# A hybrid trunk in split fp32 on one core: PSUM tiles and weights of the last plain down block, and the buffers of three norms

## The chip, the core and the metric

The kernel runs on one core of one Trainium2 chip. The metric is the device time of one execution in microseconds (us), the median of several runs. The engines are named as in the profile: PE (TensorE), PEld (PE's weight loads), DVE (VectorE), ACT (ScalarE), POOL (GpSimd) and SP (SyncE, which here issues the DMAs). A difference of 0.3% (7.3 us) is about the least that a measurement of this kernel tells from no change.

## The reference

Two layers over 1024 tokens and 16 learned meta tokens, with a model width of 1024: a token mixer (differential attention in layer 0, a gated short convolution in layer 1), then an MLP with a squared ReLU. An RMS norm stands before and after each of them.

```python
def _rmsnorm(x, g):
    y = x * lax.rsqrt(jnp.mean(x * x, axis=-1, keepdims=True) + RMS_EPS)
    return y * g

def _short_conv(h, w_in, conv_w, w_out):
    b_gate, c_gate, u = jnp.split(jnp.einsum('bld,de->ble', h, w_in), 3, axis=-1)
    u = c_gate * u
    y = lax.conv_general_dilated(u, conv_w[:, None, :], window_strides=(1,), padding=[(CONV_WIDTH - 1, 0)], ...)
    return jnp.einsum('bld,de->ble', b_gate * y, w_out)

def _sqrelu_mlp(h, w_up, w_down):
    a = jax.nn.relu(jnp.einsum('bld,df->blf', h, w_up))
    return jnp.einsum('blf,fd->bld', a * a, w_down)

    for i in range(DEPTH):
        h = _rmsnorm(hres, norm_g[i, 0])
        m = _diff_attention(...) if i % N_MIXERS == 0 else _short_conv(...)
        hres = hres + _rmsnorm(m, norm_g[i, 1])
        h = _rmsnorm(hres, norm_g[i, 2])
        hres = hres + _rmsnorm(_sqrelu_mlp(h, w_up[i], w_down[i]), norm_g[i, 3])
    return hres[:, N_META:]
```

The inner width of the MLP is 4096.

## The kernel before

**Products.** Everything lies with the features on the 128 partitions and the tokens along the free axis, so a row (`row(m, c, s)`) is one of 8 blocks of 128 features. Each fp32 operand is split in two fp32r parts, `hi` (a rounded copy) and `lo` (the rest), and a product of 128x128 weights is three matmuls: hi·hi, hi·lo, lo·hi (`product`, L180). `up` products run over 8 blocks of features (24 matmuls), `dn` products over 4 (12 matmuls). Weights are read in tiles of 128x1024 (`w_raw`, one buffer in each pool), cast to `w_hi` by ACT (L149), and `w_lo` is subtracted by DVE (L150). Tokens are worked on in three chunks, in layer 0 of 344, 344 and 340 columns (`cut0`), called chunk 0, 1 and 2 here.

**Stages.** Attention of layer 0, `project_out` (L399, products `mo`), a norm, MLP 0, a norm, the convolution's three input projections (`conv_in`, products `cg`, `ug`, `bg`), `project_out` again, a norm, MLP 1, the last norm. An MLP (`mlp`, L613 on) runs one block of four `up` tiles (`up_plain`) and writes it to DRAM, 12 pairs of `up` tiles (`up_pair`), and another plain block, whose down products open `acc`. Then `Sevens.run` makes the 6 large down blocks as seven block products each (`pa`, `pb`, `pc`) in 24 steps `q`, in each of which DVE adds seven results to `acc` (L588). A weight tile of a step is loaded two steps ahead (`fetch`), into the raw buffer of the pool `wp` for an even `q` and of `wd` for an odd one. Last comes `down_plain` for the block written to DRAM (`done0` and `done1` add its products to `acc` and sum the squares for the norm that follows).

**PSUM.** `psum_stage` sets which tiles rotate. In `psp1`, of layer 0's block products and of the last down block after them, tiles are 1024 wide, two banks each: two of `a`, one each of `b` and `c`. `down_plain` takes them in the order a, b, a, c, and the sums over partitions (`total`, a matmul with a matrix of −1) use tag `c` too. `psp2`, from `conv_in` on, has eight tiles of one bank: `mm` 2, `s` 3, `t` 2 for products and `o` for sums.

**Norms.** `norm_step` (L372) is called once per chunk when the last row of a mixer or MLP is there. PE sums the squares over partitions (`mss` or `ass`), ACT and DVE make the root's inverse (`rsqrt_mean`, L190), then for each of 8 rows: DVE scales it (L389), DVE adds the residual (L390, from tiles `st` loaded by SP, two rows each), ACT makes the `hi` part `HH` for the next product (L391), DVE the `lo` part `HL` (L392), ACT a square `sq` (L211), which POOL adds to `ssn` or `rs` for the next norm (L212). The squares for `mss` or `ass` are made the same way after each `mo` or last `dn` product. Both kinds take their `sq` from one ring of two buffers. `add` is due at once and its second sum (`close`) 15 us later on a clock that counts matmuls.

**What sets the order.** Within `Sevens.run` PE's order is that of the code. Elsewhere a scheduler places each engine's instructions by a simulated timeline and the availability of buffers, so pools and rings shift instructions against each other. After that, each engine runs its list in order, and waits where an operand is missing. 

The closing lines of a down block in layer 0 are these:

```python
    def done0(mi, cols, am, ps):
        nc.vector.tensor_add(am, am, ps)
        add_square(mp, ass[:, cols[0] : cols[0] + cols[1]], am, mi == 0, cols[1])
        if mi == KC - 1:
            norm_step(mp, 0, 3, acc, ass, cols, ...)

    down_plain(acc, *last, list(range(FB)), cut0, done0)
    psum_stage("psp2", BANKS, 512, ROUND, "o")
```

## Time and profile before

| | us |
|---|---|
| median of 3 runs | 2448.94 (2444.61 to 2450.77) |
| the profiled execution | 2453.48 |
| its span | 2451.7 |
| PE busy in it | 2358.9 |
| DVE, ACT, POOL busy | 1483.7, 996.2, 433.1 |
| mean granted clock of PE | 0.983 |

A row of the timeline reads: start, duration, engine, line, operation, out<-in by the program's names (without the numbers of buffers), shapes, how many alike follow each other, and in brackets the idle time of the engine before it and who ended it. A row of the windows reads: the stretch, its length, the busy time of PE, PEld, DVE, ACT and POOL with the number of instructions, PE's granted clock, the DMA engines' busy share and GB/s. A row of groups has a count, the busy time and mean ns of one, and the idle time before. PE runs in order, so an idle time in its rows is one in which its next instruction waited; a matmul's duration overlaps the next one's, so the pace is read from starts.

### The profile page before, as it was taken

The page shows a single profiled execution, that of the slowest core. Times are in us where ns is not written, and L with a number is a line of the kernel's source. Part 1 is how long each engine was busy: PE and PEld are TensorE (multiplying, and loading weights), DVE is VectorE, ACT ScalarE, POOL GpSimd, SP SyncE. Part 2 cuts the span into 40 slices and gives each one's busy share as a digit, 9 for nine tenths or more (in the row PEclk, how much of TensorE's full clock was granted, in tenths as well). Part 3 has the DMA queues.
Part 4 walks back from the last instruction along what each step waited for, and adds up shares of the span by engine and source line. Part 5 has one row for each costly group of instructions (what it writes and reads, how often), then busy time and mean ns, then how long its engine had stood idle before and what let it go on. Part 6 is the DMA issues. An engine that isn't in the chain of part 4 may idle for free.

```text
span 2451.7 us, 36477 instructions
## 1 busy us (share of the span) xinstructions
PE 2358.9 (96%) x14330; PEld 2215.5 (90%) x14330; DVE 1483.7 (61%) x2655; ACT 996.2 (41%) x1893; POOL 433.1 (18%) x438
## 2 busy tenths in 40 slices
PE   8999999999899999999997799999899999999997
PEld 7899999999799999999996799999788888888887
DVE  7887777764855455366666644332755555367766
ACT  7776677764533333312214422223533333222215
POOL 3211111103300000133314300002400000132316
PEclk9999999999999999999998899999999999999999
DMA  4212222333365564577542311111456555476652
GB/s 133 66 53 61 62 61 61 101 112 115 101 231 187 220 226 170 194 265 271 202 147 92 98 44 52 44 65 42 125 192 229 203 194 223 172 292 238 225 197 70
DMA packets 110108, 357.67 MB, mean 146 GB/s; under 512 B 11120, under 2 KB 55536, under 8 KB 102768
## 3 DMA queue, kind: packets, MB, share of 16 engines
q1 hardware_dynamic: 109936, 355.33, 40.9%
q8 instruction: 113, 1.85, 0.3%
q14 instruction: 59, 0.48, 0.1%
HBM read 225.94 MB, written 120.84 MB: 141 GB/s over the span
## 4 chain that ended last, share of the span: by engine, by line
PE 81%; DVE 10%; ACT 4%; issue 2%; DMA 2%; POOL 1%; SPq 0%; DVEq 0%; POOLq 0%; ACTq 0%
PE up L187 27%; PE pa L565 11%; PE pb L565 6%; PE dn L187 5%; PE mo L187 4%; PE cg L187 4%; PE ug L187 4%; PE bg L187 4%; PE pc L565 3%; PE po L1272 2%; DVE HL L392 1%; PE tr L1233 1%; PE s L1186 1%; DMA w_raw<-in_wall 1%; PE s L1187 1%
## 5 line engine op out<-in xcount | busy, mean ns | idle before, releaser
L187 PE MATMUL up<-HL,w_hi 128*128 128x344 f32 (+3 forms) x1312 | 455.9, 348 | 6.4 <-DVE HL L392 6.2
L187 PEld LDWEIGHTS up<-HL,w_hi 128*128 128x128 f32 x1312 | 248.5, 189 | 30.1 <-DVE HL L392 9.4
L150 DVE TENSOR_TENSOR w_lo<-w_raw,w_hi 128x1024 fp32r<-128x1024 f32 (+1 forms) x119 | 147.8, 1243 | 209.8 <-ACT w_hi L149 209.6
L149 ACT CAST w_hi<-w_raw 128x1024 fp32r<-128x1024 f32 (+2 forms) x143 | 148.4, 1040 | 297.4 <-PE up L187 146.8
L187 PE MATMUL up<-HH,w_hi 128*128 128x344 f32 (+1 forms) x768 | 246.7, 323 | 7.1 <-ACT HH L391 4.7
L456 DVE SCALAR_TENSOR_TENSOR r<-up,ssn 128x344 f32<-128x344 f32 (+3 forms) x164 | 92.9, 571 | 254.9 <-PE up L187 254.7
L187 PE MATMUL up<-HH,w_lo 128*128 128x344 f32 (+1 forms) x768 | 245.7, 321 | 0.0
L543 POOL TENSOR_TENSOR s_tmp<-w_raw 128x256 f32<-128x256 f32 x48 | 35.8, 747 | 1016.7 <-DMA w_raw<-in_wall 769.5
L187 PEld LDWEIGHTS up<-HH,w_hi 128*128 128x128 f32 x768 | 145.2, 189 | 8.1 <-ACT HH L391 5.3
L187 PEld LDWEIGHTS up<-HH,w_lo 128*128 128x128 f32 x768 | 145.1, 189 | 0.4 <-DVE w_lo L150 0.2
L535 ACT CAST s_hi<-s_tmp 128x1024 fp32r<-128x1024 f32 x48 | 50.4, 1049 | 162.3 <-PE pb L565 147.2
L1196 ACT ACTIVATE E<-E,mn 16x16 f32<-16x16 f32 (+5 forms) x144 | 105.3, 732 | 24.4 <-DVE mn L1191 23.7
L187 PE MATMUL up<-YHa,w_hi 128*128 128x512 f32 (+2 forms) x272 | 104.6, 386 | 4.4 <-ACT YHa L391 4.4
L212 POOL TENSOR_TENSOR mss<-mss,sq 128x344 f32<-128x344 f32 (+2 forms) x42 | 41.8, 1001 | 372.0 <-ACT sq L211 371.4
L187 PE MATMUL up<-YHa,w_lo 128*128 128x512 f32 (+2 forms) x272 | 104.7, 385 | 0.0
L187 PE MATMUL up<-YHb,w_lo 128*128 128x512 f32 (+2 forms) x272 | 103.8, 382 | 0.0
L187 PE MATMUL up<-YHb,w_hi 128*128 128x512 f32 (+2 forms) x272 | 103.4, 380 | 0.0
L187 PE MATMUL mo<-HL,w_hi 128*128 128x342 f32 (+2 forms) x312 | 99.6, 319 | 0.0
L150 POOL TENSOR_TENSOR w_lo<-w_raw,w_hi 128x1024 fp32r<-128x1024 f32 (+1 forms) x24 | 57.5, 2397 | 201.7 <-ACT w_hi L149 179.1
L1191 DVE CUSTOM_DVE_ANT_0 E<-s,G 16x16 f32<-16x16 f32 (+5 forms) x144 | 64.5, 455 | 42.9 <-PE s L1187 40.9
L588 DVE TENSOR_TENSOR acc<-acc,pa 128x512 f32<-128x512 f32 x96 | 65.9, 686 | 32.8 <-PE pa L565 31.2
L535 ACT CAST a_hi<-w_raw 128x512 fp32r<-128x512 f32 x48 | 29.7, 620 | 136.2 <-DMA w_raw<-in_wall 127.3
(498 smaller groups left out, 7292.5 us busy)
## 6 DMA issues: line engine op xcount, KB each, us to landing
w_raw<-in_wall SPq DMA_DIRECT2D x189, 512.0 KB, 3.7
seven_dram<-stage SPq DMA_DIRECT2D x12, 2056.0 KB, 6.4
seven_dram<-stage SPq DMA_DIRECT2D x12, 2048.0 KB, 6.3
fx<-seven_dram SPq DMA_DIRECT2D x42, 514.0 KB, 6.9
fx<-seven_dram SPq DMA_DIRECT2D x42, 512.0 KB, 7.0
seven_dram<-stage SPq DMA_DIRECT2D x12, 1542.0 KB, 9.3
seven_dram<-stage SPq DMA_DIRECT2D x12, 1536.0 KB, 8.7
HL<-seven_dram SPq DMA_DIRECT2D x21, 514.0 KB, 7.9
```

Of the source, the lines that this page charges most:

```text
L149: nc.scalar.copy(hi_part, raw[:, cols])
L150: (eng or nc.vector).tensor_sub(lo_part, raw[:, cols], hi_part.bitcast(F32))
L187: nc.tensor.matmul(ps, lhs[:, a:b], rhs(k, cols), start=n == 0, stop=n == last)
L212: (eng or nc.gpsimd).tensor_add(ss, ss, sq)
L456: nc.vector.scalar_tensor_tensor(r, ps, 0.0, rs[:, c0 : c0 + n], ALU.max, ALU.mult)
L535: nc.scalar.copy(hl[0], src)
L543: nc.gpsimd.tensor_add(s1, a21, a22)
L565: nc.tensor.matmul(ps[:, off : off + n], lhs[:, a : a + P], F[j][slot][:, t, c : c + n], start=first and k == 0, stop=k == 5, skip_group_c ...
L588: nc.vector.tensor_add(am, am, got)
L1191: nc.vector.tensor_tensor_reduce(out=e[:rows, p0 : p0 + n], in0=ps[:rows], in1=self.G[:rows, off : off + n], scale=-(2.0 ** -(h + 1)), sca ...
L1196: nc.scalar.activation(e[:rows, :ext], e[:rows, :ext], AF.Exp, scale=-1.0, bias=mn, accum_out=H["sums"][:rows, c : c + 1])
L1272: nc.tensor.matmul(po[:, a0:ncols], v[:, j], a[:, j, a0:ncols], start=j == 0 and z == 0, stop=j == nch - 1 and z == 2)
```

## The change

Four things, in both layers where both have them:

1. `psp2` opens before layer 0's last down block and not after it. Its `dn` products rotate over seven single banks, and the sums have the eighth.
2. The four weight tiles of the last down block are loaded and split by `take_last` in the last two steps of `Sevens.run` (two in each), in halves of 128x512, into buffers that are free by then (`a_hi`/`a_lo`, `s_tmp`, `w_hi`/`w_lo` of `wp`). The pool `wd` stays open for it until `down_plain` is through. So `wx` opens later, and `shift` sets which of the two pools the first conv weights come from. In layer 1 this is all that changes at the down block.
3. The squares made within `norm_step` have a ring of their own (tag `sqn`), apart from those of the products before. The two norms after the mixers load the residual four rows at a time (`wide` 4, two buffers), the norm after layer 0's MLP two rows at a time as before.
4. `rsq` of the convolution uses the tile `ass`, `mlp0b` lies on the right side, and closes after the convolution.

```diff
     def load_weights(eng=None, raw=None, spare=None, early=None):
-        src = wpools[max(i - 3 * HEADS - EARLY + 1, 0) // 2 % len(wpools)]
+        src = wpools[(max(i - 3 * HEADS - EARLY + 1, 0) // 2 + shift[0]) % len(wpools)]
...
     def norm_step(..., wait, wide):
-                for c2 in (c4, c4 + 2):
-                    st = tp.tile([P, 2, n], F32, tag="st", name=f"st_{count[0]}_{c2}", bufs=3)
-                    nc.sync.dma_start(st, res_in(slice(c2, c2 + 2), s))
-                    for c in (c2, c2 + 1):
+                for c2 in range(c4, c4 + 4, wide):
+                    st = tp.tile([P, wide, n], F32, tag="st", name=f"st_{count[0]}_{c2}", bufs=2 if wide == 4 else 3)
+                    nc.sync.dma_start(st, res_in(slice(c2, c2 + wide), s))
+                    for c in range(c2, c2 + wide):
...
-                        add_square(tp, ssn[:, s], mc, c == 0, n)
+                        add_square(tp, ssn[:, s], mc, c == 0, n, tag="sqn")
...
-    def down_plain(acc, fh, fl, group, chunks, done):
-        ws = [weights() for _ in group]
+    def down_plain(acc, fh, fl, group, chunks, done, ws=None):
+        ws = ws or [[(w, 0), (w, FB * P)] for w in [weights() for _ in group]]
...
+        def take_last(self, i):
+            _, raw = self.take(4 * NW + i)
+            halves = [slice(0, 4 * P), slice(4 * P, 8 * P)]
+            def half(t):
+                return self.wd.tile([P, 4 * P], F32R, tag=f"a_{t}", name=f"last_{t}{i}_{count[0]}", bufs=3)
+            if i == 1:
+                ws = [[half("hi"), half("lo")] for _ in halves]
+            elif i == 3:
+                hi = self.wd.tile([P, 1024], F32R, tag="s_tmp", name=f"last_hi{count[0]}", bufs=1)
+                ws = [[hi[:, s], half(t)] for s, t in zip(halves, ("hi", "lo"))]
+            else:
+                w = [wp.tile([P, 1024], F32R, tag=f"w_{t}", name=f"last_{t}{i}_{count[0]}") for t in ("hi", "lo")]
+                ws = [[t[:, s] for t in w] for s in halves]
+            for w, s in zip(ws, halves):
+                self.split(w, raw[:, s])
+            self.last.append([(w, 0) for w in ws])
...
                 for q in range(n + 1):
                     if q + 2 < n:
                         self.fetch(q + 2)
+                    elif q == n - 1:
+                        self.take_last(0)
+                        self.take_last(1)
+                    elif q == n:
+                        self.take_last(2)
+                        self.take_last(3)
...
-        wds.close()
         reopen()
-        wxp[0] = ctx.enter_context(ExitStack())
-        wpools.append(wxp[0].enter_context(pool("wx", 2)))
-        return acc, base_plain
+        return acc, base_plain, seven.last, wds
...
+    psum_stage("psp2", BANKS, 512, ROUND, "o")
     second = ctx.enter_context(ExitStack())
-    mp = second.enter_context(pool("mlp0b", 1))
+    mp = second.enter_context(pool("mlp0b", 1, "right"))
...
-    down_plain(acc, *last, list(range(FB)), cut0, done0)
-    psum_stage("psp2", BANKS, 512, ROUND, "o")
+    down_plain(acc, *last, list(range(FB)), cut0, done0, ws)
+    wds.close()
+    wxp[0] = ctx.enter_context(ExitStack())
+    wpools.append(wxp[0].enter_context(pool("wx", 2)))
+    shift[0] = 1
...
-    rsq = cp.tile([P, T1], F32, name="rsq")
+    rsq = ass
```

The change moves instructions that the diff doesn't show. The first place is POOL at the first norm after a mixer, where the squares are added up. Before (`mss` sums the squares of the mixer's rows, `ssn` those of the normed rows; 128x344 with `sq` from 7232 to 7319 are of chunk 1, 128x340 of chunk 2):

```order
L212 TENSOR_TENSOR mss_6833<-mss_6833,sq_7319 128x344
L212 TENSOR_TENSOR ssn_6834<-ssn_6834,sq_7341 128x344
L212 TENSOR_TENSOR ssn_6834<-ssn_6834,sq_7350 128x344
L212 TENSOR_TENSOR ssn_6834<-ssn_6834,sq_7357 128x344
L212 TENSOR_TENSOR ssn_6834<-ssn_6834,sq_7367 128x344
L212 TENSOR_TENSOR ssn_6834<-ssn_6834,sq_7374 128x344
L212 TENSOR_TENSOR ssn_6834<-ssn_6834,sq_7383 128x344
L212 TENSOR_TENSOR ssn_6834<-ssn_6834,sq_7390 128x344
L212 TENSOR_TENSOR mss_6833<-mss_6833,sq_7420 128x340
L212 TENSOR_TENSOR mss_6833<-mss_6833,sq_7457 128x340
L212 TENSOR_TENSOR mss_6833<-mss_6833,sq_7486 128x340
L212 TENSOR_TENSOR mss_6833<-mss_6833,sq_7515 128x340
```

After:

```order
L212 TENSOR_TENSOR mss_6833<-mss_6833,sq_7315 128x344
L212 TENSOR_TENSOR ssn_6834<-ssn_6834,sq_7177 128x344
L212 TENSOR_TENSOR ssn_6834<-ssn_6834,sq_7184 128x344
L212 TENSOR_TENSOR mss_6833<-mss_6833,sq_7412 128x340
L212 TENSOR_TENSOR ssn_6834<-ssn_6834,sq_7191 128x344
L212 TENSOR_TENSOR mss_6833<-mss_6833,sq_7449 128x340
L212 TENSOR_TENSOR ssn_6834<-ssn_6834,sq_7198 128x344
L212 TENSOR_TENSOR mss_6833<-mss_6833,sq_7478 128x340
L212 TENSOR_TENSOR mss_6833<-mss_6833,sq_7507 128x340
L212 TENSOR_TENSOR ssn_6834<-ssn_6834,sq_7337 128x344
L212 TENSOR_TENSOR ssn_6834<-ssn_6834,sq_7344 128x344
L212 TENSOR_TENSOR ssn_6834<-ssn_6834,sq_7351 128x344
```

The four adds of chunk 2's `mss` stood behind the seven of chunk 1's `ssn` (7341 to 7390); now they stand ahead of them, among those of chunk 0. On PE the sum of chunk 2's `mss` moves with them, from behind 178 `up` matmuls to behind 80 (in layer 1 from about 165 to 82), and that of chunk 1 from behind some 22 `up` matmuls to 36 matmuls ahead of the last `mo`.

The second place is DVE in layer 0's last down block, at the end of its chunk 2 (128x340), while the norm of a chunk of 128x344 runs. Before (L695 adds a `dn` product to `acc0`, L390 and L392 are of the norm of chunk 1, L150 splits a conv weight):

```order
L392 SCALAR_TENSOR_TENSOR HL_13893<-acc0a,g,HH 128x344
L390 TENSOR_TENSOR acc0b<-acc0b,st_6_14321 128x344 x2
L392 SCALAR_TENSOR_TENSOR HL_13893<-acc0a,g,HH 128x344
L392 SCALAR_TENSOR_TENSOR HL_13893<-acc0b,g,HH 128x344
L736 TENSOR_TENSOR rsq<-rs_13901 128x344
L392 SCALAR_TENSOR_TENSOR HL_13893<-acc0b,g,HH 128x344 x2
L695 TENSOR_TENSOR acc0a<-acc0a,dn_14378 128x340
L392 SCALAR_TENSOR_TENSOR HL_13893<-acc0b,g,HH 128x344
L150 TENSOR_TENSOR w_lo_14569<-w_raw_14566,w_hi_14568 128x1024
L695 TENSOR_TENSOR acc0b<-acc0b,dn_14446 128x340
```

After (L725 is the add to `acc0`; the norm in these rows is that of chunk 0 up to the last L392, and that of chunk 1 from L196 on):

```order
L392 SCALAR_TENSOR_TENSOR HL_13915<-acc0b,g,HH 128x344
L725 TENSOR_TENSOR acc0a<-acc0a,dn_14394 128x340
L392 SCALAR_TENSOR_TENSOR HL_13915<-acc0b,g,HH 128x344
L725 TENSOR_TENSOR acc0b<-acc0b,dn_14428 128x340
L725 TENSOR_TENSOR acc0b<-acc0b,dn_14411 128x340
L150 TENSOR_TENSOR w_lo_14567<-w_raw_14564,w_hi_14566 128x1024
L725 TENSOR_TENSOR acc0b<-acc0b,dn_14445 128x340
L196 SCALAR_TENSOR_TENSOR q_14267<-sum_14265,q_14267 128x344
L725 TENSOR_TENSOR acc0b<-acc0b,dn_14462 128x340
L197 SCALAR_TENSOR_TENSOR ass_13923<-q_14267,ass_13923 128x344
L389 SCALAR_TENSOR_TENSOR acc0a<-acc0a,g,ass_13923 128x344 x4
```

The last two adds of chunk 2 stood behind nearly all of chunk 1's norm; now all of them but one stand ahead of that norm's first operation.

The third is PE at the sum of chunk 2's `ass`. Before:

```order
L187 MATMUL dn_14446<-HL,w_hi_13922 128x340 x2
L187 MATMUL dn_14446<-HL,w_lo_13923 128x340
L203 MATMUL sum_14480<-ass_13900,minus 128x340
L187 MATMUL cg_14578<-HH,w_hi_14562 128x344
L187 MATMUL cg_14578<-HL_13893,w_hi_14562 128x344
```

After:

```order
L187 MATMUL cg_14644<-HL_13915,w_hi_14572 128x344
L187 MATMUL cg_14644<-HH,w_lo_14573 128x344
L187 MATMUL cg_14671<-HL_13915,w_hi_14560 128x344
L187 MATMUL cg_14671<-HH,w_lo_14561 128x344
L203 MATMUL sum_14479<-ass_13923,minus 128x340
L187 MATMUL cg_14671<-HH,w_hi_14560 128x344
```

The sum stood right behind the last `dn` product, ahead of every conv product; now the three conv products of chunk 0 and the start of chunk 1's first (`cg_14671`) stand ahead of it. The sum of chunk 1 stood ahead of the last two `dn` products and stands within the last three now; that of chunk 2 follows it after 95 rows instead of 18.

More of the change, by code (lines that the diff above doesn't have):

```diff
@@ L370, in last_step, with norm_step @@
         return [partial(finish, a, b, nc.vector if dve else nc.gpsimd) for a, b, dve in CUTS]
-    def norm_step(tp, layer, which, m, mss, cols, res_in, res_out, nxt, H, L, ssn, wait):
+    def norm_step(tp, layer, which, m, mss, cols, res_in, res_out, nxt, H, L, ssn, wait, wide):
         c0, n = cols
@@ L500, in down_plain @@
             s = slice(c0, c0 + n)
-            for gi, w in zip(group, ws):
-                for half in range(2):
+            for gi, halves in zip(group, ws):
+                for half, (w, w0) in enumerate(halves):
                     mi = 2 * gi + half
@@ L517, in __init__ @@
             self.F, self.W, self.raw = [base, None], {}, {}
+            self.last = []
         def load(self, b, slot):
@@ L529, in fetch @@
             self.raw[q] = raw
+            return i, raw
+        def take_last(self, i):
[14 more added lines that the diff above has]
+            self.last.append([(w, 0) for w in ws])
+        def fetch(self, q):
+            i, raw = self.take(q)
             a = [self.wd.tile([P, 4 * P], F32R, tag=f"a_{t}", name=f"a_{t}{i}", bufs=3) for t in ("hi", "lo")]
@@ L767, in trunk @@
     conv_pool.close()
+    second.close()
     h2.close()
@@ L788, in trunk @@
             [sevens(HL, h)[:, k] for k in range(7)]]
-    acc, last = mlp(1, yh, yl, ssn, h, two1, base, last_quarters(*YH, SEQ), fine, cut1, third,
+    acc, last, ws, _ = mlp(1, yh, yl, ssn, h, two1, base, last_quarters(*YH, SEQ), fine, cut1, third,
                     ("psp3", {"a": 3, "b": 2, "c": 2, "o": 1}, 512, ["a", "b", "c", "a", "b", "c", "a"], "o"), lambda: None)
@@ L827, in done1 @@
             sqs.clear()
-    down_plain(acc, *last, list(range(FB)), tail, done1)
+    down_plain(acc, *last, list(range(FB)), tail, done1, ws)
     for step in steps:
```

17 lines of the change are left out of this document (8 added, 9 removed).

## The prediction

> **What bounds the kernel now.** I read the page's busy times first, then its chain that ended last.
>
> ```profile
> PE 2358.9 (96%) x14330; PEld 2215.5 (90%) x14330; DVE 1483.7 (61%) x2655; ACT 996.2 (41%) x1893; POOL 433.1 (18%) x438
> ...
> PE 81%; DVE 10%; ACT 4%; issue 2%; DMA 2%; POOL 1%; SPq 0%; DVEq 0%; POOLq 0%; ACTq 0%
> ```
>
> PE is busy for all but 92.8 of the 2451.7 us of the span, so only two things can shorten the run without taking work away: PE's waits, and the slow clock that follows them. I therefore took PE's timeline from the first post-mixer norm on and kept the rows with idle time before them. They lie in four places, and the windows of three of them (the fourth is the start of layer 1's last down block) show what is lost there (columns: PE, PEld, DVE, ACT, POOL busy, granted clock, DMA share, GB/s):
>
> ```profile
> 611.70:675.00 63.30, 53.23 (x301) 49.49 (x300) 54.52 (x93) 32.19 (x69) 21.64 (x20) 0.92 0.30 98
> 1278.40:1413.60 135.20, 103.81 (x589) 98.33 (x589) 85.28 (x141) 54.58 (x110) 45.66 (x42) 0.86 0.32 102
> 1325.00:1366.00 41.00, 13.47 (x43) 10.22 (x43) 26.22 (x41) 18.89 (x38) 24.08 (x22) 0.61 0.38 120
> 1729.86:1793.10 63.24, 53.58 (x301) 49.86 (x300) 54.70 (x92) 31.68 (x68) 21.07 (x20) 0.92 0.31 98
> ```
>
> The second is layer 0's last down block, its norm and the first conv products; in its 41 us from 1325 PE works 13.5 us at a clock of 0.61. First and fourth are the two norms after the mixers, with the `up` products that wait for them.
>
> **Layer 0's last down block.** The ideal first. These two rows are the same place in two neighbouring `dn` products, one product of 12 matmuls apart:
>
> ```profile
> 1297.13 0.47 PE L187 MATMUL dn<-HL,w_hi 128*128 128x344 f32 x2
> ...
> 1299.02 0.48 PE L187 MATMUL dn<-HL,w_hi 128*128 128x344 f32 x2
> ```
>
> 1.89 us for 12 matmuls, 0.1575 each. The window holds 24 `dn` products (45.4), 12 conv products of 24 matmuls (9 `cg`/`ug`, 3 `bg`: 45.4) and six sums of two matmuls (about 2): 92.8 us. It takes 135.2, so 42.4 are lost. The waits are these:
>
> ```profile
> 1278.94 0.91 PE L187 MATMUL dn<-HL,w_hi 128*128 128x344 f32 x4 [0.52 <-ACT w_hi L149]
> 1280.99 0.43 PE L187 MATMUL dn<-HL,w_lo 128*128 128x344 f32 x1 [1.14 <-DVE w_lo L150]
> 1287.48 0.90 PE L187 MATMUL dn<-HL,w_hi 128*128 128x344 f32 x4 [1.22 <-ACT w_hi L149]
> 1288.74 0.42 PE L187 MATMUL dn<-HL,w_lo 128*128 128x344 f32 x1 [0.36 <-DVE w_lo L150]
> ...
> 1289.47 0.75 PE L187 MATMUL dn<-HL,w_hi 128*128 128x344 f32 x2
> ...
> 1325.76 0.58 PE L187 MATMUL dn<-HL,w_hi 128*128 128x340 f32 x2 [1.38 <-DVE acc0a L695]
> ...
> 1334.34 1.51 PE L203 MATMUL sum<-ass,minus 128*128 128x344 f32 x2 [6.44 <-POOL ass L212]
> 1338.08 1.52 PE L203 MATMUL sum<-rs,minus 128*128 128x344 f32 x2 [2.23 <-DVE q L196]
> 1345.22 0.94 PE L187 MATMUL dn<-HL,w_hi 128*128 128x340 f32 x2 [5.62 <-DVE q L196]
> ...
> 1354.55 0.93 PE L187 MATMUL dn<-HL,w_hi 128*128 128x340 f32 x2 [5.56 <-DVE acc0a L695]
> ...
> 1365.03 1.50 PE L203 MATMUL sum<-ass,minus 128*128 128x340 f32 x2 [6.92 <-POOL ass L212]
> ```
>
> They add up to 31.4 us; the other 11.0 are slow clock (two matmuls take 0.75 instead of 0.48 at 1289.47), 0.35 us for each us of waiting. The first four, 3.2 us, are late weights. All later ones have one cause. With four PSUM tiles, and the sums in the tag of one of them, a `dn` product waits until DVE has added an older one to `acc0`, and DVE does this behind a norm; meanwhile PE holds no conv product that it could do, because `psp2` opens only when the block is through.
>
> Afterwards seven single banks rotate and the sums have the eighth. Counting the seven products' end as 0: chunks 0 and 1 give 16 products, 30.2 us, and each add must be done only when the seventh product behind it begins, 13 us later. An add costs 0.51, and the worst stretch ahead of it in the new order is about half a norm. So I price the four bank waits (1.38, 5.62, 5.56, and 2.23 at the sum of `rs`) at nothing: what hides them is seven products of 1.89. The POOL waits (6.44, 6.92) go because the sum of chunk 1 now stands near the end of the `dn` products, and that of chunk 2 in conv products of chunk 1 (rows in the part on the change). What is late next is the norm itself. Its length now is from the end of the sum to the last `HL`:
>
> ```profile
> 1354.42 0.80 DVE L392 SCALAR_TENSOR_TENSOR HL<-acc0b,g,HH 128x344 fp32r<-128x344 f32 x1
> ...
> 1384.34 0.56 DVE L392 SCALAR_TENSOR_TENSOR HL<-acc0b,g,HH 128x340 fp32r<-128x340 f32 x1
> ```
>
> 1355.2 − 1335.9 = 19.4 us for chunk 1 and 1384.9 − 1366.5 = 18.4 for chunk 2. In the new order PE reaches the sum of chunk 1 behind some 22 `dn` products (41.6); I put it at 43, as POOL's adds for it end about then. With all `dn` products (45.4), the three conv products of chunk 0 (11.3) and three sums (1.0) PE comes to the rows of chunk 1 at 57.7. These end at 43 + 19.4 = 62.4 at best, and up to 69 as DVE now also drains chunk 2 and splits conv weights: PE waits row by row for 1.5 to 5.5 us, I take 4. The sum of chunk 2 follows at about 60, its rows end at 80 to 89, and until 85 PE has other products. The rest behind the last row is half a product of 3.78 and the group's last three or so, so the place ends at 97 to 102.
>
> The weights: their load, cast and subtraction (8 half subtractions instead of 4 whole ones) go into the block products' last two steps, where DVE's adds of block products must wait behind them.
>
> ```profile
> w_raw<-in_wall SPq DMA_DIRECT2D x189, 512.0 KB, 3.7
> ...
> L536 DVE TENSOR_TENSOR a_lo<-w_raw,a_hi 128x512 fp32r<-128x512 f32 x24 | 19.7, 821 | 13.2 <-ACT a_hi L535 13.1
> ...
> 1286.38 1.04 ACT L149 CAST w_hi<-w_raw 128x1024 fp32r<-128x1024 f32 x1 [7.49 <-DMA w_raw<-in_wall]
> ```
>
> Eight halves are 6.6 us of DVE. With only two raw buffers the third and fourth weight are loaded when the first two are split; 3.7 us of transfer is mostly covered by the remaining block products. From below this costs nothing, from above a whole transfer of 3 us left open; I take 1.2, nearer to nothing, because the load goes out some ten us before the end.
>
> Sum: 92.8 + 1.2 + 4, and 0.35 × 5.2 = 1.8 of slow clock: 99.8 against 135.2, a gain of **35** (27 to 39).
>
> On the clock the Trainium skill, page "TensorE: Matmul & The Clock Gate", Part 1, says that PE falls to half rate only after an idle window of about 3.4 us. By it the short waits that I leave would cost no clock, and the gain would be 37. Here the trace agrees only in part: 1289.47 is slow after waits of 1.22 and 0.36.
>
> **The two norms after the mixers.** Before, in PE's rows of both and POOL's of the first:
>
> ```profile
> 615.63 0.85 PE L203 MATMUL sum<-mss,minus 128*128 128x344 f32 x2 [0.26 <-POOL mss L212]
> ...
> 641.94 0.42 PE L187 MATMUL up<-HH,w_hi 128*128 128x344 f32 x1 [2.33 <-DVE r L456]
> ...
> 653.55 1.22 PE L187 MATMUL up<-HH,w_hi 128*128 128x340 f32 x3 [4.73 <-ACT HH L391]
> 656.60 0.65 PE L187 MATMUL up<-HL,w_hi 128*128 128x340 f32 x1 [1.83 <-DVE HL L392]
> ...
> 665.63 0.42 PE L187 MATMUL up<-HL,w_hi 128*128 128x340 f32 x1 [0.40 <-DVE HL L392]
> ```
>
> ```profile
> 1762.63 0.84 PE L203 MATMUL sum<-mss,minus 128*128 128x340 f32 x2 [1.34 <-POOL mss L212]
> 1771.26 0.93 PE L187 MATMUL up<-YHa,w_hi 128*128 128x340 f32 x2 [4.38 <-ACT YHa L391]
> ```
>
> ```profile
> 603.75 4.01 POOL L212 TENSOR_TENSOR ssn<-ssn,sq 128x344 f32<-128x344 f32 x3 [1.64 <-ACT sq L211]
> 607.73 1.92 POOL L212 TENSOR_TENSOR mss<-mss,sq 128x344 f32<-128x344 f32 x2
> ...
> 637.94 3.15 POOL L212 TENSOR_TENSOR mss<-mss,sq 128x340 f32<-128x340 f32 x3
> 643.36 1.06 POOL L212 TENSOR_TENSOR mss<-mss,sq 128x340 f32<-128x340 f32 x1 [2.27 <-ACT sq L211]
> ```
>
> The 288 `up` matmuls are 45.4 us and the sums 2.2: 15.7 of 63.3 us are lost. The last wait is for chunk 2's norm. Its sum could not start before 644.4, since POOL took the adds to `mss` after those to `ssn` of the chunk before. With rings of their own the squares no longer queue like this: the sum of chunk 2 stands behind 80 `up` matmuls instead of 178, 98 × 0.1575 = 15.4 us of PE's work earlier; that of chunk 1 some 9 us earlier. DVE sets the limit: it is busy for 54.5 of the 63.3 us, and its norm of chunk 2 can't start before that of chunk 1 is through. Chunk 1's sum comes at about 606; its norm of 19.4 is held up, by my estimate for 6 us, by ACT's cast of an `up` weight whose load (3.7 us) goes out at about 607 in the new order. Its last row is then due at 632, chunk 2's near 653.5 instead of 665.6, and the products left over take some 10 us as now (675.0 − 665.6): 664 to 666 against 675. Gain **10** (6 to 14). The larger `st` tiles halve the loads there, off the path. Layer 1's place has the same rows and lost 15.6; its sum moves from behind about 165 matmuls to behind 82, so **10** again.
>
> **Layer 1's last down block.**
>
> ```profile
> 2383.93 0.38 PE L187 MATMUL dn<-YHa,w_hi 128*128 128x256 f32 x1 [0.45 <-ACT w_hi L149]
> ...
> 2390.56 0.39 PE L187 MATMUL dn<-YHa,w_hi 128*128 128x256 f32 x1 [0.55 <-ACT w_hi L149]
> ```
>
> Only 1.0 us can be gained; the same splits as in layer 0 could cost 2. I take **0.5** gained (−2 to +1).
>
> **The sum.** 35 + 10 + 10 + 0.5 = 55.5. The profiled execution took 2453.5 us, 1.7 more than its span, so 2398; it lies 4.5 above the median of 2448.9, and for a median I take **2394**. With the four ranges (37 to 68): 2381 to 2412.
>
> **Rivals.**
>
> *DVE and POOL become the bound.* All three norms run closer together, with drains between.
>
> ```profile
> L392 DVE SCALAR_TENSOR_TENSOR HL<-acc0b,g,HH 128x344 fp32r<-128x344 f32 x8 | 6.8, 875 | 0.0
> ...
> L695 DVE TENSOR_TENSOR acc0b<-acc0b,dn 128x344 f32<-128x344 f32 x8 | 4.1, 507 | 4.4 <-PE dn L187 4.4
> ...
> L212 POOL TENSOR_TENSOR ass<-ass,sq 128x344 f32<-128x344 f32 (+1 forms) x21 | 22.2, 1056 | 42.1 <-ACT sq L211 41.1
> ```
>
> The subtraction with two SBUF operands takes 0.56 alone (1384.34) and 0.88 in the mean beside POOL, the add from PSUM 0.51 always. If each of a norm's 24 such operations (0.54) waited out its share of 14 POOL adds (0.93), a norm took 13 + 13 = 26 us and not 19: two norms behind each other, 13 less gained at the down block, and 6 less at each of the others. Gain 30, **2419**. For it: DVE's 54.5 of 63.3. Against: norms beside POOL are in the 19 already. The Trainium skill, page "SBUF — State Buffer", section "Who interferes with whom", has this as a rule: such a DVE instruction and a reading GpSimd one share a port under an exclusive lock. The mean of 875 ns agrees, but a full block each time is not seen. Chance 0.15.
>
> *The norms' waits only move* (to the weights' cast or the row loads): the down block alone, 35, **2414**. Against it stands POOL's order, for it that DVE is nearly full. 0.13.
>
> *Everything goes, the slow clock too*: 42.4 + 15.7 + 15.6 + 1.0 = 75, **2374**. It needs a norm of under 15 us (43 + 15 = 58, when PE reaches its rows). 0.07.
>
> *Slower: the late weights stop the block products.* ACT waited 7.49 us for a `w_raw`. If all four transfers of a layer stood open in DVE's queue with drains of block products behind them, PE would lose 4 × 7.5 × 2 = 60 and 21 of clock: 81 − 55.5 = 25 more, **2474**. It decides from 55.5 / (8 × 1.35) = 5.1 us per weight. Against: transfers run ahead of the splits by a step. 0.05.
>
> *The edit does nothing on PE's path*, since a wait as long takes each one's place: 2449. The order of the instructions speaks against it. 0.04.
>
> **Chances.** My forecast 0.56. A measurement here can tell 0.3%, 7.3 us, from no change: faster 0.91, within 0.04, slower 0.05. The range takes in forecast and the first two rivals, 2381 to 2420.
>
> **What would show it.** Right: at the down block PE waits under 7 us in all, at 0.95 of the clock or more, none for a bank; the place takes 97 to 102 us; the mixers' norms take 50 to 57 each, and the wait of 4 to 5 us for `HH` is gone or below 2. Wrong: waits on `acc0` or on POOL stay, block products wait near the end of the sevens, or the mean of L392 (its line number after) rises above 0.95 and the rows of a chunk come more than 22 us behind its sum.

## The result, and the profile after

The change runs in 2403.59 us (median of 4 runs, 2403.25 to 2407.89) against 2449.69 for the kernel before (4 runs): a ratio of 0.982, 95% interval 0.9802 to 0.9838, 46.1 us faster. The forecast was 2394, with 2381 to 2420 as its range. The profiled execution took 2403.25, its span 2401.1.

The page of the kernel after, busy times and chain:

```profile
PE 2342.2 (98%) x14330; PEld 2202.7 (92%) x14330; DVE 1485.9 (62%) x2663; ACT 996.4 (41%) x1901; POOL 445.3 (19%) x438
...
PE 81%; DVE 11%; ACT 3%; issue 2%; DMA 2%; SPq 0%; DVEq 0%; ACTq 0%
```

PE's idle time fell from 92.8 to 58.9 us, and POOL is gone from the chain, where it had 1%. POOL has the same 438 instructions and is busy for 12 us more: its adds have become longer, which comes up again below.

The windows of the three places, and two pieces of the second (columns as before: PE, PEld, DVE, ACT, POOL busy, granted clock, DMA share, GB/s):

```profile
606.50:664.20 57.70, 51.97 (x305) 48.87 (x304) 54.56 (x96) 31.38 (x64) 19.46 (x16) 0.97 0.32 103
1267.60:1372.60 105.00, 98.14 (x589) 95.25 (x589) 85.40 (x138) 52.76 (x109) 46.52 (x42) 0.97 0.38 122
1300.00:1325.00 25.00, 23.15 (x140) 21.62 (x138) 23.58 (x33) 14.69 (x31) 19.01 (x17) 1.00 0.49 167
1325.00:1345.00 20.00, 16.85 (x93) 16.17 (x94) 19.97 (x33) 13.04 (x28) 8.27 (x7) 0.91 0.61 194
1689.30:1743.90 54.60, 49.51 (x299) 46.60 (x298) 51.63 (x91) 31.68 (x65) 18.01 (x16) 1.00 0.33 107
```

The first norm takes 57.7 instead of 63.3 (its window holds six later matmuls, 0.9 us, and one sum less than the one before), the down block with its norm 105.0 instead of 135.2, the second norm 54.6 instead of 63.2. At both norms DVE is now busy for 95% of the stretch, and at the down block for nearly all of 1300 to 1345.

What PE still waits for, in its timeline of the kernel after: the first two rows of the block are of the first norm, then one of the block products, five of the down block, three of the second norm.

```profile
610.20 0.82 PE L203 MATMUL sum<-ssn,minus 128*128 128x344 f32 x2 [1.79 <-DVE q L196]
631.97 1.21 PE L203 MATMUL sum<-ssn,minus 128*128 128x344 f32 x2 [2.75 <-DVE q L196]
...
1263.04 0.50 PE L591 MATMUL pa<-fx,s_hi 128*128 128x258 f32 x2 [0.68 <-DVE acc0b L614]
...
1308.98 0.58 PE L187 MATMUL dn<-HL,last_hi 128*128 128x340 f32 x2 [0.66 <-DVE acc0a L725]
1313.65 0.58 PE L187 MATMUL dn<-HL,last_hi 128*128 128x340 f32 x2 [0.56 <-DVE acc0a L725]
...
1326.23 0.42 PE L187 MATMUL cg<-HH,w_hi 128*128 128x344 f32 x1 [1.61 <-ACT HH L391]
1328.89 0.66 PE L187 MATMUL cg<-HH,w_lo 128*128 128x344 f32 x1 [1.92 <-DVE w_lo L150]
...
1347.85 0.42 PE L187 MATMUL cg<-HH,w_hi 128*128 128x340 f32 x1 [1.86 <-ACT HH L391]
...
1693.38 0.81 PE L203 MATMUL sum<-ssn,minus 128*128 128x342 f32 x2 [0.92 <-DVE q L196]
...
1713.00 0.81 PE L203 MATMUL sum<-ssn,minus 128*128 128x342 f32 x2 [1.26 <-DVE q L196]
...
1729.20 0.42 PE L187 MATMUL up<-HL,w_hi 128*128 128x340 f32 x1 [1.53 <-DVE HL L392]
```

No wait at the down block is longer than 1.92, the two POOL waits of over 6 us are gone, the bank waits have shrunk to 0.66 and 0.56. The releaser is DVE nearly everywhere. At the norms a wait that was not there before has come: the second sum (`ssn`) stands in PE's order until DVE has read the first one out of their common bank, which DVE does behind norm rows.

To compare the kernels below I cut each trace at places that all have: from the start of `mo`'s last group in layer 0 to the end of layer 0's block products (A: the first norm and what follows it), from there to the last group of `mo` in layer 1 (B: the down block, its norm, the convolution, whose part behind the window above took 270.6 us before and after), from there to the first `up` of 512 columns (C: the second norm), and to the end of PE's last matmul (D: layer 1's MLP). Before, A took 712.3, B 405.8, C 108.8, D 646.8. What lies ahead of A, where nothing was changed, was 2.5 to 7.3 us shorter in all later profiles than in the one of before, which goes with the 4.5 us by which this one was above its median. The differences to the profile of before, in us gained:

| kernel | median us | A | B | C | D |
|---|---|---|---|---|---|
| the change | 2403.6 | 5.0 | 30.3 | 8.0 | 1.7 |
| psum_alone | 2435.7 | −1.5 | 12.4 | 0.8 | −0.3 |
| rings_alone | 2431.8 | 6.2 | 4.0 | 8.1 | −1.4 |
| no_psum | 2425.7 | 2.0 | 8.4 | 8.3 | 1.7 |
| no_weights | 2407.7 | 5.7 | 28.1 | 8.2 | 0.2 |
| no_ring | 2429.9 | 0.6 | 15.9 | −0.4 | 1.7 |
| no_pool_adds | 2380.8 | 14.7 | 37.9 | 15.0 | 1.7 |
| no_residual | 2399.2 | 6.8 | 33.2 | 7.9 | 1.8 |
| two_sum_banks | 2403.5 | 4.9 | 31.6 | 7.3 | 1.7 |
| adds_on_dve | 2389.3 | 14.3 | 27.9 | 15.1 | 1.7 |
| adds_on_pe | 2386.5 | 12.3 | 35.3 | 13.2 | 1.7 |
| dve_norms_pe_down | 2384.9 | 14.3 | 35.8 | 15.1 | 1.7 |
| pe_and_dve | 2390.8 | 12.2 | 33.5 | 13.2 | 1.7 |

In `no_psum`, as in layer 1, `dn` products stand among the last block products, so its boundary between A and B is blurred; its A and B together gained 10.4. A single profile's A moves by 1 to 1.5 us where nothing was changed (`psum_alone`).

### The profile page after: what moved, and what is told of

The parts are those of the page before. It is cut to its first block, busy times and chain, and to the rows that moved or that the text cites. A ratio compares the mean times of both kernels' runs of the same rounds, so it can differ in the third digit from the quotient of the medians.

```text
span 2401.1 us, 36496 instructions
## 1 busy us (share of the span) xinstructions
PE 2342.2 (98%) x14330; PEld 2202.7 (92%) x14330; DVE 1485.9 (62%) x2663; ACT 996.4 (41%) x1901; POOL 445.3 (19%) x438
## 4 chain that ended last, share of the span: by engine, by line
PE 81%; DVE 11%; ACT 3%; issue 2%; DMA 2%; SPq 0%; DVEq 0%; ACTq 0%
PE up L187 27%; PE pa L591 11%; PE dn L187 5%; PE pb L591 5%; PE mo L187 4%; PE bg L187 4%; PE ug L187 3%; PE cg L187 3%; PE pc L591 3%; PE po L1305 2%; DVE HL L392 2%; PE s L1219 1%; PE tr L1266 1%; PE s L1220 1%; PE q L972 1%
## 5 line engine op out<-in xcount | busy, mean ns | idle before, releaser
L150 DVE TENSOR_TENSOR w_lo<-w_raw,w_hi 128x1024 fp32r<-128x1024 f32 (+1 forms) x111 | 137.2, 1237 | 189.0 <-ACT w_hi L149 188.9
L149 ACT CAST w_hi<-w_raw 128x1024 fp32r<-128x1024 f32 (+2 forms) x135 | 140.3, 1040 | 260.2 <-PE up L187 153.5
L212 POOL TENSOR_TENSOR mss<-mss,sq 128x344 f32<-128x344 f32 (+2 forms) x42 | 50.1, 1198 | 375.8 <-ACT sq L211 366.8
L1229 ACT ACTIVATE E<-E,mn 16x16 f32<-16x16 f32 (+5 forms) x144 | 105.3, 732 | 23.9 <-DVE mn L1224 23.4
L150 POOL TENSOR_TENSOR w_lo<-w_raw,w_hi 128x1024 fp32r<-128x1024 f32 (+1 forms) x24 | 57.5, 2394 | 196.7 <-ACT w_hi L149 174.1
```

The costliest lines, as they stand in the source:

```text
L149: nc.scalar.copy(hi_part, raw[:, cols])
L150: (eng or nc.vector).tensor_sub(lo_part, raw[:, cols], hi_part.bitcast(F32))
L212: (eng or nc.gpsimd).tensor_add(ss, ss, sq)
L1229: nc.scalar.activation(e[:rows, :ext], e[:rows, :ext], AF.Exp, scale=-1.0, bias=mn, accum_out=H["sums"][:rows, c : c + 1])
```

## The experiments

### The parts by themselves

`psum_alone` is the kernel before with one line moved:

```diff
     HL2 = held["L"]
+    psum_stage("psp2", BANKS, 512, ROUND, "o")
...
     down_plain(acc, *last, list(range(FB)), cut0, done0)
-    psum_stage("psp2", BANKS, 512, ROUND, "o")
```

> The kernel before with one edit: psp2 opens ahead of layer 0's last down block. Theory A (each part stands for itself, and the PSUM tiles are the cause of the waits at the down block): the four bank waits and both POOL waits at the sums go, 28 us and some 8 of slow clock of which DVE gives back part; gain 24 to 30, so about 2422; the mixers' norms stay as they were. Rival B (the sums wait for POOL because the squares of a running norm are ahead in the shared ring, so the tiles alone only move the wait): the waits of 6.4 and 6.9 at the sums stay, gain 10 to 15, about 2437.

2435.74 (2433.69 to 2438.47) against 2447.39, a ratio of 0.9952 (0.9937 to 0.9967): 11.7 gained, 12.4 at B. PE's timeline of this kernel at the down block:

```profile
1332.26 0.85 PE L203 MATMUL sum<-ass,minus 128*128 128x344 f32 x2 [0.48 <-POOL ass L212]
1340.96 0.65 PE L187 MATMUL cg<-HH,w_hi 128*128 128x344 f32 x1 [4.28 <-ACT HH L391]
1344.04 0.66 PE L187 MATMUL cg<-HL,w_hi 128*128 128x344 f32 x1 [1.86 <-DVE HL L392]
...
1361.64 1.50 PE L203 MATMUL sum<-ass,minus 128*128 128x340 f32 x2 [3.45 <-POOL ass L212]
1365.36 1.51 PE L203 MATMUL sum<-rs,minus 128*128 128x344 f32 x2 [2.21 <-DVE q L196]
1370.93 0.65 PE L187 MATMUL cg<-HH,w_hi 128*128 128x340 f32 x1 [4.06 <-ACT HH L391]
```

Of the four bank waits three are gone, as theory A had it, and 2.21 at the sum of `rs` stays. Most of the time is not gone: the sum of chunk 1 comes 56.9 us behind the end of the block products (1275.4), in the change 42.9 (1310.5 against 1267.6). POOL's adds for it still queue behind the squares of chunk 0's norm, so chunk 1's and 2's rows are late, and PE waits 4 us for each. Theory A falls. B stands with 11.7 (10 to 15), though of the waits at the sums of `ass` that it expected to stay only one does, with 3.45.

`rings_alone` undoes the PSUM part and the early weights in the change and keeps ring and row loads:

```diff
-    psum_stage("psp2", BANKS, 512, ROUND, "o")
     second = ctx.enter_context(ExitStack())
...
     down_plain(acc, *last, list(range(FB)), cut0, done0, ws)
+    psum_stage("psp2", BANKS, 512, ROUND, "o")
...
-                    elif q == n - 1:
-                        self.take_last(0)
...
```

> Of the change only the norms' own ring and the four-row loads (with the layout of the pools that these need); PSUM and the weights of the last down block as before. Theory A: 6 us gained at the first mixer norm and 8 at the second as in the full change, nothing at the down block: about 2435. Rival B: the POOL waits at the down block shrink as well, another 5 to 10: about 2428.

2431.83, a ratio of 0.9935 (0.9921 to 0.995), 15.6 gained: A and C have all that they have in the change, B 4.0. That lies between theory A (2435) and rival B (2428, with 5 to 10 at the down block). The waits at its down block:

```profile
1319.63 1.52 PE L203 MATMUL sum<-ass,minus 128*128 128x344 f32 x2 [7.44 <-POOL ass L212]
...
1330.51 0.94 PE L187 MATMUL dn<-HL,w_hi 128*128 128x340 f32 x2 [5.62 <-DVE q L196]
1339.85 0.93 PE L187 MATMUL dn<-HL,w_hi 128*128 128x340 f32 x2 [5.57 <-DVE acc0a L721]
1348.85 1.50 PE L203 MATMUL sum<-ass,minus 128*128 128x340 f32 x2 [5.24 <-POOL ass L212]
```

With four tiles the ring alone does little there: the waits of before stay. So neither part does it alone, 12.4 and 4.0 at B, but both together do (`no_weights`: 28.1). 11.7 us belong to the pair.

`no_psum` takes only the PSUM part back; `no_weights` only the early weights (`take_last` isn't called, `down_plain` loads its weights, `wx` opens ahead of it as before).

> The change without its PSUM part (psp2 opens behind the last down block again). Theory A: 14 from the rings, 3 from the weights of layer 0 and 1.7 of layer 1: about 2431. Rival B, by which tiles and rings are needed together: the same, or lower by what the rings bring at the down block alone, to 2425.

> The change without the early weights (loaded and split at the head of the last down block again, wx open as before). Theory A: the 3.2 us of weight waits come back with 1 of clock, and 1.7 at layer 1's block, less 0.9 that the block products lost: about 2408.5, at the down block's head two pairs of waits for w_hi and w_lo. Rival (the early weights cost as much as they bring, in DVE's queue ahead of the norm): 2403 to 2405.

`no_psum` took 2425.68, a ratio of 0.9912 (0.9898 to 0.9927). Against `rings_alone` it adds the early weights and has 0.2 more at A and B together and 3.1 at D: with four tiles the weights that are there earlier only lead to the next wait sooner. The time is near the lower end of what rival B had (2425). The medians are 6.1 apart, though, and the profiled execution of `no_psum` was the slowest of its four, 3.3 above their median, so its trace may show too little. `no_weights` took 2407.66 (2404.87 to 2409.69), a ratio of 0.9839 (0.9823 to 0.9856), whose interval overlaps the change's, so the times alone don't settle it; the traces do. Its waits at the head of the down block:

```profile
1266.55 0.58 PE L187 MATMUL dn<-HL,w_hi 128*128 128x344 f32 x2 [0.52 <-ACT w_hi L149]
1267.46 0.89 PE L187 MATMUL dn<-HL,w_hi 128*128 128x344 f32 x4 [0.33 <-DVE acc0b L614]
...
1275.33 1.20 PE L187 MATMUL dn<-HL,w_hi 128*128 128x344 f32 x6 [0.40 <-ACT w_hi L149]
```

Of the 3.2 us before, 0.92 stay as waits for weights, and 0.33 is one for an add of the block products. I take it that with seven banks PE goes on with other products while a weight is late. The early weights bring 2.2 at B and 1.5 at D and cost 0.7 at A (the wait of 0.68 for `acc0b` among the block products): 3.0 net.

`no_ring` takes the tag `sqn` back and nothing else:

```diff
-                        add_square(tp, ssn[:, s], mc, c == 0, n, tag="sqn")
+                        add_square(tp, ssn[:, s], mc, c == 0, n)
```

> The change without the norms' own ring (their squares again in the ring of the products' squares); tiles, early weights and four-row loads as in the change. Theory A2 (the tiles help at the down block only as far as POOL's adds for the next sum are not queued behind a norm's squares): the place gives 14 to 18 us instead of 30, the mixers' norms nothing, about 2430, with POOL waits at the sums of the down block. Rival (additive parts): the place gives 26, about 2421.

2429.91, a ratio of 0.9921 (0.9904 to 0.9937). B gains 15.9, A 0.6, C nothing: theory A2. The POOL waits that I expected at its sums are not there, though; the timeline shows what stands in their place:

```profile
1336.62 0.66 PE L187 MATMUL cg<-HH,w_hi 128*128 128x344 f32 x1 [3.82 <-ACT HH L391]
...
1365.00 0.65 PE L187 MATMUL cg<-HH,w_hi 128*128 128x340 f32 x1 [4.36 <-ACT HH L391]
```

The scheduler has put the sums where their squares are ready, and PE waits for the rows behind them. So one edit of a tag is worth 26 us with the tiles and early weights, and it is what both norms gain; the four-row loads have no share in it that this run shows.

### What is left

The change left some 9, 12 and 7 us at the three places above the work that PE has there (47.6, 92.8, 47.6), and DVE was full. Theory C: DVE is the bound, slowed by POOL. Two kernels leave work out.

```diff
-            (eng or nc.gpsimd).tensor_add(ss, ss, sq)
+            if tag == "sq":
+                (eng or nc.gpsimd).tensor_add(ss, ss, sq)
```

> The change, leaving out POOL's adds of the squares made within the norms (the second norm's sum of squares holds one row only); ACT still makes the squares. Theory C (what is left at the three places is DVE, full and slowed by POOL): the means of L392, L390 and L197 fall to 0.51 to 0.57, DVE's busy time falls by 6 to 8 us at each mixer norm and 8 to 12 at the down block, and PE gets most of it: 5, 5 and 7 less, about 2387. Rival (PE waits for its order and for latency, not for DVE's load): DVE's times fall, PE's windows hardly do, 2399 or more.

```diff
-                        nc.vector.tensor_add(mc, mc, st[:, c - c2])
```

> The change, leaving out the residual adds (L390) of the three norms: 24 DVE instructions less at each place, some 14 us of DVE. Theory C: PE's loss at the places shrinks by 5 to 9 each, about 2383. Rival (order and latency): the rows come earlier by 4 us per chunk but PE gains 2 or less at each, about 2398.

`no_pool_adds` took 2380.82 (2 runs), 22.8 less than the change, more than expected: nearly all the loss of the three places is gone. `no_residual`, with 24 DVE instructions less at each place, took 2399.24 (2 runs), 4.4 less. The subtraction to `HL` on DVE, in the view of one line's instructions (count, then min/median/max in ns), of the change:

```profile
L392 DVE SCALAR_TENSOR_TENSOR HL<-m0a,g,HH x12: 564/1240/1290, 592.5 to 646.9; 128x344 fp32r<-128x344 f32 x8, 128x340 fp32r<-128x340 f32 x4
```

of `no_pool_adds` (the line's number is one higher):

```profile
L393 DVE SCALAR_TENSOR_TENSOR HL<-m0a,g,HH x12: 564/573/1239, 593.9 to 636.7; 128x344 fp32r<-128x344 f32 x8, 128x340 fp32r<-128x340 f32 x4
```

The same for the scaling of a row (L389), first in the change, then in `no_residual`:

```profile
L389 DVE SCALAR_TENSOR_TENSOR m0b<-m0b,g,mss x12: 564/565/568, 587.2 to 636.5; 128x344 f32<-128x344 f32 x8, 128x340 f32<-128x340 f32 x4
```

```profile
L389 DVE SCALAR_TENSOR_TENSOR m0b<-m0b,g,mss x12: 562/900/1245, 589.7 to 637.1; 128x344 f32<-128x344 f32 x8, 128x340 f32<-128x340 f32 x4
```

Without POOL's adds the subtraction's median falls from 1.24 to 0.57, and PE has no wait left at either mixer norm, although the sums stand where they stand in the change (at the first norm the later ones behind 12, 81 and 116 `up` matmuls, in the change behind 11, 80 and 115). So it is POOL that makes these waits, and not the order. Of theory C this half stands.

The other half, that DVE's own work is the bound, `no_residual` doesn't settle. Its time is the rival's 2398 and not theory C's 2383. The norms become shorter (at the down block chunk 1's takes 20.8 us from the end of its sum to the last row, in the change 27.7), although POOL's adds now meet the scaling too: its median goes from 0.57 to 0.90 for the rows `m0b`, and the subtraction stays at 1.23. But the scheduler has also put the sums elsewhere, at the first norm that of chunk 0's `ssn` among the last `mo` products, and PE's waits there are now at the sums (2.19, 1.56 and 1.64).

The Trainium skill, page "SBUF — State Buffer", section "Who interferes with whom", says that a DVE instruction with two SBUF inputs contends with a GpSimd instruction that reads SBUF. These rows agree. The subtraction grows by 0.7, and a POOL add alone takes 0.93; the last section shows how the two take turns.

`two_sum_banks` asks whether the new waits at the sums are a cause of their own:

```diff
-    psum_stage("psp2", BANKS, 512, ROUND, "o")
+    psum_stage("psp2", {"mm": 2, "s": 3, "t": 1, "o": 2}, 512, ["mm", "s", "t", "mm", "s", "s"], "o")
```

> The change with two banks for the sums and six for the products in psp2 (down block, convolution, layer 1's norm after the mixer). Theory D (a second sum in PE's order waits until DVE has read the first one's bank, PE stands behind it): the waits at the sums of 0.9 and 1.3 in layer 1 go, 2 gained there, the down block as before: about 2401.5. Theory C (DVE is full there): the time moves to waits on HL or r, within 1 of 2403.6, and six banks cost 0 to 2 at the down block.

2403.53, the change's time: B gained 1.3, C lost 0.7. With a second bank the wait at `ssn`'s first sum of the second norm is gone, and waits for `HL` stand there instead, as theory C had it. Those waits are symptoms.

### Versions that take POOL out of DVE's way

If an add on POOL costs DVE as much as it costs POOL, it may as well run on DVE, or PE can sum the squares itself.

```diff
-                        add_square(tp, ssn[:, s], mc, c == 0, n, tag="sqn")
+                        add_square(tp, ssn[:, s], mc, c == 0, n, eng=nc.vector, tag="sqn")
```

> The change with the adds of the norms' squares on DVE in place of POOL. Theory E (a POOL add holds back DVE's instructions with two SBUF operands for about as long as it runs, so an add on DVE costs DVE no more than one on POOL): L392 falls to 0.56, DVE's busy time at each place stays within 4 us of the change's although it has 21 instructions of 0.51 more there, and the time stays within 2396 to 2406. Rival (POOL's adds run beside DVE and cost it little): 10.7 us more of DVE at each of three places that are DVE-bound, 2425 or more.

2389.29, a ratio to before of 0.9756 (0.9739 to 0.9774): 14.3 less than the change, better than either theory had it. The window from `mo`'s last group to the end of the first norm's `up` products, of the change and of this kernel:

```profile
560.30:664.30 104.00, 98.27 (x596) 94.77 (x596) 78.21 (x126) 55.35 (x116) 48.28 (x39) 0.98 0.32 100
```

```profile
558.70:653.40 94.70, 94.70 (x597) 93.52 (x596) 72.57 (x141) 54.94 (x114) 24.26 (x18) 1.00 0.34 109
```

Both stretches hold the same work of PE. The 21 adds cost DVE 11.7 us; its 24 subtractions `HL` take 14.1 us instead of 23.9, and the six operations of L197 3.1 instead of 5.3. So DVE has 21 instructions more and is no busier, and PE has no idle time and a full clock. Both norms gain about what they gained without the adds (14.3 and 15.1; there 14.7 and 15.0). The order of the sums has moved here too (chunk 1's `ssn` stands behind 195 `up` matmuls instead of 115), so this run alone wouldn't tell POOL from the order; `no_pool_adds` does, and `adds_on_pe` below, with its sums behind 25, 86 and 123, has no wait there either. The down block loses 2.4 against the change: there DVE has the drains and the conv weights as well, and its timeline shows waits for these.

```profile
1313.16 0.45 PE L187 MATMUL cg<-HH,w_hi 128*128 128x344 f32 x1 [2.06 <-ACT w_hi L149]
1316.96 0.66 PE L187 MATMUL cg<-HH,w_lo 128*128 128x344 f32 x1 [1.06 <-DVE w_lo L150]
1338.25 0.65 PE L187 MATMUL cg<-HH,w_hi 128*128 128x340 f32 x1 [4.08 <-ACT HH L391]
```

`adds_on_pe` gives the last squares to PE (four rows at the mixers' norms, three at the down block):

```diff
+                        if c < KC - (4 if wide == 4 else 3):
                             add_square(tp, ssn[:, s], mc, c == 0, n, tag="sqn")
+                        else:
+                            sq = tp.tile([P, n], F32R, tag=f"sqd{c}", name=f"sqd_{count[0]}_{c}", bufs=1)
+                            nc.scalar.activation(sq, mc, AF.Square)
+                            direct.append(sq)
...
+        for i, ss in enumerate(direct):
+            nc.tensor.matmul(ps, minus_r, ss, start=False, stop=i == len(direct) - 1)
```

> The change with part of the squares summed by PE itself: the last four rows' squares of the mixers' norms and the last three of the norm at the down block are written as fp32r and go as further operands into the second sum, 4 x 3 and 3 x 3 matmuls of 0.16 us at a place, and as many POOL adds fall away; the loads of st at the down block have two buffers instead of three for room. Theory E: of the 23 us that went with all POOL adds, 4/7 at the norms and 3/7 at the down block come back, 12.7, less 5.2 of matmuls: about 2396. Rival (the loss is in the order of the sums, not in POOL's adds): 5 slower, 2409.

2386.46, a ratio of 0.9742 (0.9728 to 0.9757): 17.1 less than the change, where 7.5 were expected. The down block gains 35.3, 5.0 more than in the change, with three of seven adds gone. Its granted clock stays at 1.00 at all three places, where the change has three stretches of half clock (in the next section).

The last two combine them: `dve_norms_pe_down` has DVE's adds at the mixers' norms, and at the down block three squares on PE and the rest on POOL; `pe_and_dve` is `adds_on_pe` with its remaining adds on DVE.

> The change with what did best at each place: the norms after the mixers add their squares on DVE, the norm at the down block gives its last three rows' squares to PE as fp32r and the others to POOL. If the places stand for themselves (theory E): 10.3 less at the first norm, 7.0 at the second and 5.0 at the down block than in the change, 2381. If they depend on each other: 2386 or more.

> adds_on_pe with its remaining adds (three of seven rows at the mixers' norms, four at the down block) on DVE in place of POOL, so that POOL adds nothing within the norms. Theory E: at the mixers' norms no wait is left, the matmuls cost 1.9 each, 13 gained there against before; at the down block DVE's adds delay the rows, 33 to 36 against before; 2383 to 2388. Rival (without POOL beside it DVE is no longer the bound anywhere): 37 at the down block, 2382 or less.

`dve_norms_pe_down` took 2384.86 (2382.19 to 2385.38), a ratio of 0.9732 (0.9716 to 0.9749): 18.7 us below the change and 64.9 below the kernel before. By its places it is where the parts put it (A 14.3, B 35.8, C 15.1; the parts have 14.3, 35.3 and 15.1). The 10.3 expected at the first norm was 1.0 too much, since the start of A in `adds_on_dve` had been read that much too late. The median lies between the 2381 expected and the 2386 of the rival, and its profile had 3 us more ahead of A than the change's. It is the fastest of all complete kernels here; the ratio of `adds_on_pe` is within its interval. Its granted clock is 1.00 from A to the end of D but for the last 5 us. Its waits at the down block:

```profile
1318.13 0.43 PE L189 MATMUL cg<-HH,w_hi 128*128 128x344 f32 x1 [0.61 <-ACT HH L397]
1319.93 0.42 PE L189 MATMUL cg<-HH,w_lo 128*128 128x344 f32 x1 [1.07 <-DVE w_lo L152]
...
1337.42 0.42 PE L189 MATMUL cg<-HH,w_hi 128*128 128x340 f32 x1 [1.22 <-ACT HH L397]
```

`pe_and_dve` took 2390.81, a ratio of 0.976 (0.9745 to 0.9774): 33.5 at the down block, within its 33 to 36, and 4.4 more in all than `adds_on_pe` and 2.8 over the upper end of what was expected. Of the 3.6 by which the two profiles differ only 1.8 are at the down block, where the granted clock is at half once (1340.1 to 1343.5) and in `adds_on_pe` never; 1.6 lie ahead of A, where nothing differs. With the 2.4 of `adds_on_dve` it still looks as if at the down block the adds are better on POOL than on DVE, so that the exchange is not one for one there. I take the reason to be that POOL's adds also fall beside DVE's drains, which take 0.49 to 0.52 whether POOL runs or not; no run shows it by itself.

## Why the prediction was right, and where it wasn't

**Sign and size.** Forecast 54.9 below the median of before, measured 46.1. The terms were 35, 10, 10 and 0.5; the traces have 30.3, 5.0 (5.9 at the norm itself, less 0.9 in the block products), 8.0 and 1.7. The first norm (6 to 14) and layer 1's last block (−2 to 1) each lie about 1 us outside their own ranges, the other two terms inside.

**The down block: right in size, wrong in its cause.** The prediction gave the PSUM tiles the bank waits and POOL waits alike, and the ring only the norms after the mixers. The tiles alone bring 12.4, the ring alone 4.0, both 28.1. The sentence that failed is that the POOL waits go "because" the sums stand later in PE's order. The sum of chunk 1 stands behind 264 `dn` matmuls before and behind 265 in the change; that of chunk 2 does move, behind 77 of the convolution. With the tiles alone both stand later than in either, behind all 288 `dn` matmuls and 53 and 144 of the convolution, and still PE waits 3.45 for POOL at the second, and the rest goes over into 4.3, 1.9 and 4.1 for the rows of chunks 1 and 2. What freed the sum is POOL's order. These are POOL's adds ahead of it, before and in the change:

```profile
1321.74 4.31 POOL L212 TENSOR_TENSOR rs<-rs,sq 128x344 f32<-128x344 f32 x3 [0.35 <-ACT sq L211]
1326.02 8.26 POOL L212 TENSOR_TENSOR ass<-ass,sq 128x344 f32<-128x344 f32 x7
```

```profile
1301.77 1.22 POOL L212 TENSOR_TENSOR ass<-ass,sq 128x344 f32<-128x344 f32 x1
1302.93 1.22 POOL L212 TENSOR_TENSOR rs<-rs,sq 128x344 f32<-128x344 f32 x1
1304.11 1.22 POOL L212 TENSOR_TENSOR ass<-ass,sq 128x344 f32<-128x344 f32 x1
```

Before, all seven adds to `rs` stood ahead of all seven to `ass`; with a ring of their own they take turns. (In `rings_alone` they take turns too, but there the products that feed them wait for the four tiles, and PE waits 7.44 at the sum.) So POOL's adds there were queued in the same way as at the norms, and I applied that reading to two places of three. The four bank waits, priced at nothing, cost 1.2. The end of the block products cost 0.7 where I took 1.2. The term that was too small is the norm: I let it take 19.4 us, up to 26, and it takes 27.7 for chunk 1 and 25.6 for chunk 2 (20.6 and 19.2 in `no_pool_adds`). So chunk 1's rows end at 71.4 and not by 69, and the place ended 105 us behind its start; the forecast was 99.8, with 97 to 102 as the mark for being right. The last mark for being wrong, a mean of L392 above 0.95 with rows more than 22 us behind their sum, came true in its second half at this place (the mean is 0.87), and in both at the first norm (1.05, and 29.5 us).

**The norms: right in mechanism, too large.** The sums moved as stated, and the waits of 4.7 and 4.4 for `HH` are gone. What was left out is the next wait: the second sum, ahead in PE's order, waits for DVE to read the first (1.79 and 2.75; 0.92 and 1.26). I had named DVE's 54.5 of 63.3 us as the limit and then let 19.4 us per norm stand, although the two norms would now meet more of POOL's adds. The first norm's last two chunks take 29.5 and 28.3 us (20.7 and 20.3 before); there L392's median was 1.21 and 0.57 in the two halves of its rows before, and is 1.24 and 1.23 now.

**The clock.** I used 0.35 us of slow clock for each us of waiting. The granted clock follows no such rate: in these traces it is 1.00, or 0.50 for 3.4 us or a multiple of that. Before, it was 0.50 from 1330.4 to 1357.8. In the change it is so twice at the down block, of which this is the first, and once at the first norm (632.3 to 635.7):

```profile
1328.60:1332.00 3.40, 3.11 (x11) 3.11 (x12) 3.40 (x6) 2.34 (x6) 3.17 (x3) 0.50 1.05 351
```

Waits of 1.61 and 1.92 lie mostly in the 3.4 us ahead of it, so no single wait need be 3.4 long; at the second norm, with waits up to 1.53, the clock stays at 1.00. Each such stretch costs about 1.7 us. Of the loss left at the down block (12.2 us) 6.9 are idle, some 3.4 slow clock, and the other 1.9 neither, as at the second norm, where 1.9 of 7.0 are not idle. Part of that, by my estimate, is that a matmul's shown duration (0.32) is longer than its pace (0.16), so that a wait costs a little more than the idle time it shows.

**The first rival** (DVE and POOL become the bound, 2419) was right in mechanism and too high by 15 us. Its norm of 26 us is near the 27.7 and 25.6 measured; what PE loses by it was priced too high. It is what separates 2403.6 from the 2380.8 that the same kernel has without the adds; I gave it 0.15 as an alternative, and it was a part of the outcome. The rival on the slower side, late weights that stop the block products, cost 0.7.

**Layer 1's down block.** 1.7 instead of 0.5: the two waits of 1.0 in all went, and the splits cost nothing there. The other 0.7 is no slow clock, which was 1.00 there before too.

## What to carry over

When two uses share a ring of buffers, the later use's work can queue behind the earlier one's on the engines that follow, here on POOL; look for it at each place where the ring is used, and not only where its wait is longest. A part's share is not what it gives alone: tiles and ring gave 12 and 4 us apart and 28 together. And work put on an engine that looks idle (POOL at 19%) may be paid for by another one: compare an instruction's fastest and median time in the same trace before counting it as free.
